# A hybrid decoder step on one core: the sampled tokens' heads in the second token group, earlier fast steps, prefetched head outputs and later pair stores

## The chip, the core and the metric

The kernel runs on one core of a Trainium2 chip. It is one program. Its metric is the device time of one execution in microseconds, as the median of several runs. The core has five engines that run at the same time and wait for each other through semaphores: TensorE (PE in the profile; its weight loads are a row of their own, PEld), VectorE (DVE), ScalarE (ACT), GpSimd (POOL) and SyncE (SP). Each of them works its instructions off in order. SyncE, ScalarE and GpSimd can also issue DMA transfers.

## The reference

One layer of a decoder over 2048 prompt tokens (one sequence) and 8 x 4 sampled tokens with a state of their own, in f32, with a width of 1024:

```python
xn = rms_norm(x, norm_mix_pre)
qk_raw, v_m, o_m, gates, q_a, k_a, v_a = split_projection(xn @ w_in)   # 2312 columns
qk, conv_new = short_conv(qk_raw, conv_buf, conv_w)                    # 4 taps, then silu
# mLSTM heads (4), chunks of 128: matrix memory c, normaliser n, running maximum m
# sliding-window heads (8, in 2 groups of keys), window 128, learned sinks, ALiBi
y_m = mlstm_output(h, o_m, mlstm_norm)
y_a = rms_norm(att, attn_norm)
x = x + rms_norm(concat(y_m, y_a) @ w_out, norm_mix_post)
f = square(relu(rms_norm(x, norm_ffn_pre) @ w_up)) @ w_down            # 4096 wide
x = x + rms_norm(f, norm_ffn_post)
x = x + sigmoid(x @ w_pgate) * (p @ w_pproj)
```

The prompt starts from an empty state. The sampled tokens start from the given state of 8 sequences: c (8 x 4 x 64 x 128), n (8 x 4 x 64), m, the last three rows of the convolution, and caches of 128 keys and values. All outputs and all new states are returned.

## The kernel before

**Numbers.** Each f32 operand of a large matmul is split into a high part and a low part (`split`, `wsplit`: a copy on ScalarE that rounds, then a subtraction on VectorE or GpSimd), and a product is three matmuls, high x high, high x low and low x high (`mm3`). The sampled tokens, 32 rows, have both parts side by side in one operand and need two (`mm2s`).

**Stages.** First the input projection with both kinds of heads, over six chunks of the prompt (`CHUNKS`: four of three blocks of 128 tokens, two of two blocks). The sampled tokens are projected with the last chunk and kept in DRAM (`zsd`). A chunk goes through `gv` (gates, keys and values of the window heads), `qa`, `qk`, `v`, `o`; its mLSTM and window heads run as side work beside the following projections (`mlstm_chunk`, `swa_chunk`) and leave their results in DRAM, `yd`. Then three groups of two chunks each (`GROUPS`) go through output projection (`mix_load`, `mix_mm`, `mix_post`), MLP (`mlp`) and gate (`gate_embed`, `gate_post`, `gate_mm`). The sampled tokens ride along with the last group.

**The MLP.** It has 16 steps of 256 hidden units (`STEPS`). In a plain step `up` takes 96 matmuls for both chunks; in a fast step (`s >= FAST[gi]`, `up_both`) seven products of sums and differences of operand blocks take the place of eight, 84 matmuls. Fast steps need sums of the activations (`sums`, `last_sum`, seven VectorE operations and three splits for each half of the columns), made in step `FAST[gi] - 1`. That step also ends the sampled tokens' heads: `pe.drain(dec)`.

**Weights.** `Ring` hands out weight tiles in the order of one long plan. A tile's f32 data are loaded by SyncE to a raw tile (5 buffers) and split into a pair of high and low part (7 buffers, `PAIRS`). If the plan needs it again, the pair is stored to DRAM by a DMA that GpSimd issues (`keep`), and later loaded back ready-made by SyncE (`get`). In the profile a raw tile is `wr`, a block of `w_up` for the products `wb`, a pair `w`, its copy in DRAM `wk`.

**Order.** TensorE's order is written out: `Flow` keeps a model time of matmuls, and generators (`Side`) emit the next piece of side work when the model time has passed what they yielded; `drain` runs a side to its end. All of TensorE's instructions are held in that order. On the other engines a list scheduler with its own estimates decides the order, so an instruction whose inputs seem ready may be put before earlier ones; `keep_in_program_order` holds one instruction behind the engine's instruction traced before it.

**The sampled tokens' heads.** `decode` is a side of its own: `decode_mlstm`, then `decode_swa`. It is added before the first group's MLP, waits `DECW` = 20 us of model time, and issues its loads from ScalarE (`fetch_small`), one for each of 8 parts of c and 8 of n (L1211, L1212), then bias, queries, keys, values and sinks for the window part (L1259 to L1272). n moves in elements of 4 bytes, in and out (L1254). The two copies of the caches (L1089) are issued by SyncE. The tanh of the output gate is L1226.

**Other places that the change touches.** `fetch` loads and norms the next chunk's tokens (`row_rstd`, L497 to L499; `norm_x`, L584). `weights` in `mlstm_chunk` adds the causal mask to a row that comes back from DRAM (L902, L903). `transpose_x` turns tokens (L149, `ident`), and `split` follows (L227, L228). L1683 adds a `down` product to `f`, L1681 copies the first one, L1647 and L1573 are the sums and the relu of `up`, L1486 and L1488 the evacuation of the output projection, L1392 to L1406 the row norms behind it. `finish` ends in the store L1765.

## Time and profile before

| what | value |
|---|---|
| median of 3 runs | 2689.13 us (2686.86 to 2690.82) |
| the profiled execution | 2687.73 us, its span 2685.6 us |
| mean granted TensorE clock | 0.980 |
| busy: PE, DVE, ACT, POOL | 2546.3, 1473.3, 981.4, 613.3 us |
| moved by DMA | 626.97 MB, mean 233 GB/s |
| input projection with heads | 0 to about 690 us |
| first group: output projection, MLP, gate | from 693, 797 and 1373 us |
| second group: the same | from 1479, 1549 and 2059 us |
| third group: the same | from 2158, 2216 and 2597 us |

All times are us from the start of the span; PE is TensorE's matmuls, an engine's name with q its issuing of DMAs and waits. A row `A <- B: t, n, l` says that A stood t us in total, n times, at the longest l, until B was done. Rows of one line are told apart by tile names: `mo` is the output projection, `up` and `dn` the MLP, `pg` and `pv` the gate, tiles beginning with `dp` and `da` the sampled tokens' heads.

### The profile page before, as it was taken

The page shows a single profiled execution, that of the slowest core. Times are in us where ns is not written, and L with a number is a line of the kernel's source. Part 1 is how long each engine was busy: PE and PEld are TensorE (multiplying, and loading weights), DVE is VectorE, ACT ScalarE, POOL GpSimd, SP SyncE. Part 2 cuts the span into 40 slices and gives each one's busy share as a digit, 9 for nine tenths or more (in the row PEclk, how much of TensorE's full clock was granted, in tenths as well). Part 3 has the DMA queues.
Part 4 walks back from the last instruction along what each step waited for, and adds up shares of the span by engine and source line. Part 5 has one row for each costly group of instructions (what it writes and reads, how often), then busy time and mean ns, then how long its engine had stood idle before and what let it go on. Part 6 is the DMA issues. An engine that isn't in the chain of part 4 may idle for free.

```text
span 2685.6 us, 39181 instructions
## 1 busy us (share of the span) xinstructions
PE 2546.3 (95%) x14282; PEld 2216.1 (83%) x14282; DVE 1473.3 (55%) x3109; ACT 981.4 (37%) x2163; POOL 613.3 (23%) x894
## 2 busy tenths in 40 slices
PE   6899999999878999999989999999999998999997
PEld 6788878887657788888878888899988878999986
DVE  5675756755554486566663474444446345444453
ACT  4555444544433443334452352222223133222241
POOL 5311111112323156566651113000001010000010
PEclk9899999999889999999989999999999999999999
DMA  8756656667977366666589865555556886777786
GB/s 284 275 200 197 208 175 220 210 212 250 287 247 156 133 218 244 235 235 235 227 301 323 322 213 182 187 190 189 188 189 224 293 327 215 255 259 256 258 293 227
DMA packets 225336, 626.97 MB, mean 233 GB/s; under 512 B 35233, under 2 KB 71445, under 8 KB 225128
## 3 DMA queue, kind: packets, MB, share of 16 engines
q1 hardware_dynamic: 173424, 466.78, 52.2%
q0 software_dynamic: 44176, 154.25, 14.8%
q10 hardware_dynamic: 7544, 3.44, 0.6%
q8 instruction: 113, 1.85, 0.3%
q14 instruction: 79, 0.65, 0.1%
HBM read 470.22 MB, written 155.25 MB: 233 GB/s over the span
## 4 chain that ended last, share of the span: by engine, by line
PE 72%; DMA 9%; DVE 8%; issue 4%; POOL 3%; ACT 3%; ACTq 0%; SPq 0%; POOLq 0%; DVEq 0%
PE up L145 19%; PE dn L145 19%; PE pg L145 6%; PE mo L145 4%; PE v L145 3%; PE o L145 2%; PE qk L145 2%; DMA wk<-w 2%; PE gv L145 2%; POOL w L249 2%; PE pv L145 1%; PE aT L149 1%; PE aO L145 1%; DMA w<-wk 1%; PE qa L145 1%
## 5 line engine op out<-in xcount | busy, mean ns | idle before, releaser
L145 PE MATMUL dn<-w,hh 128*128 128x512 f32 x1792 | 567.7, 398 | 14.1 <-DVE f L1683 8.9
L145 PEld LDWEIGHTS dn<-w,hh 128*128 128x128 f32 x1792 | 332.7, 189 | 96.7 <-DVE f L1683 15.4
L1683 DVE TENSOR_TENSOR f<-f,dn 128x512 f32<-128x512 f32 x420 | 285.7, 686 | 218.0 <-PE dn L145 217.7
L145 PE MATMUL dn<-w,hl 128*128 128x512 f32 x896 | 354.3, 395 | 0.1
L1647 DVE TENSOR_TENSOR re<-up,re 128x384 f32<-128x384 f32 (+1 forms) x280 | 144.1, 515 | 297.6 <-PE up L145 297.6
L145 PEld LDWEIGHTS dn<-w,hl 128*128 128x128 f32 x896 | 168.9, 189 | 39.9 <-DVE hl L228 0.6
L268 POOL DMA_DIRECT2D wk<-w x242 | 134.1, 555 | 145.6 <-DVE w L249 109.6
L1648 ACT COPY re<-up 128x384 f32<-128x384 f32 (+1 forms) x40 | 17.9, 448 | 383.1 <-PE up L145 383.1
L228 DVE TENSOR_TENSOR hl<-re,hh 128x384 fp32r<-128x384 f32 (+1 forms) x192 | 117.5, 612 | 65.6 <-ACT hh L227 62.0
L1573 ACT ACTIVATE re<-re 128x384 f32<-128x384 f32 (+1 forms) x160 | 78.8, 493 | 179.3 <-DVE re L1647 177.2
L248 ACT CAST w<-wb 128x512 fp32r<-128x512 f32 x98 | 60.8, 621 | 199.2 <-PE dn L145 124.9
L248 ACT CAST w<-wr 128x512 fp32r<-128x512 f32 (+1 forms) x152 | 93.4, 619 | 104.9 <-issue 30.8
L249 POOL TENSOR_TENSOR w<-wr,w 128x512 fp32r<-128x512 f32 (+1 forms) x76 | 102.0, 1342 | 81.8 <-ACT w L248 62.8
L1394 POOL TENSOR_TENSOR f<-f,gffn 128x512 f32<-128x512 f32 x16 | 21.0, 1319 | 415.4 <-ACT j L1392 415.2
L249 POOL TENSOR_TENSOR w<-wb,w 128x512 fp32r<-128x512 f32 x70 | 89.9, 1295 | 100.8 <-ACT w L248 100.3
L249 DVE TENSOR_TENSOR w<-wr,w 128x512 fp32r<-128x512 f32 (+1 forms) x76 | 80.5, 1061 | 44.4 <-ACT w L248 42.4
L1574 ACT ACTIVATE re<-re 128x384 f32<-128x384 f32 (+1 forms) x192 | 94.8, 494 | 5.9
L1002 DVE CUSTOM_DVE_ANT_0 s<-aS,cst,sink 128x256 f32<-128x256 f32 (+1 forms) x128 | 57.1, 472 | 72.4 <-PE aS L145 72.2
L145 PE MATMUL up<-ut00h,w 128*128 128x384 f32 x320 | 88.6, 348 | 8.4 <-ACT f L1681 5.0
L227 ACT CAST hh<-re 128x384 fp32r<-128x384 f32 (+1 forms) x192 | 92.4, 482 | 6.8
L145 PE MATMUL up<-ut01h,w 128*128 128x384 f32 x320 | 89.8, 343 | 4.8 <-ACT re L1573 4.8
L1008 ACT ACTIVATE s<-s,swt 128x257 f32<-128x257 f32 (+1 forms) x128 | 63.3, 496 | 71.6 <-DVE swt L1005 70.4
(1501 smaller groups left out, 6436.3 us busy)
## 6 DMA issues: line engine op xcount, KB each, us to landing
w<-wk SPq DMA_DIRECT2D x678, 512.0 KB, 4.6
wk<-w POOLq DMA_DIRECT2D x238, 512.0 KB, 5.7
wr<-in_w_down_dram SPq DMA_DIRECT2D x64, 256.0 KB, 5.9
wb<-in_w_up_dram SPq DMA_DIRECT2D x28, 512.0 KB, 3.9
w<-wk SPq DMA_DIRECT2D x20, 528.0 KB, 4.2
x<-in_x_prompt_dram SPq DMA_DIRECT2D x16, 512.0 KB, 4.1
xr<-in_x_prompt_dram SPq DMA_DIRECT2D x16, 512.0 KB, 12.7
y<-yd SPq DMA_DIRECT2D x32, 256.0 KB, 6.2
```

Source lines behind the costliest of these rows:

```text
L145: ins = self.pe.matmul(out, lhsT, rhs, start=start, stop=stop)
L227: act.copy(hi, src)
L228: dve.tensor_tensor(lo, src, hi.bitcast(F32), ALU.subtract)
L248: act.copy(hi, src)
L249: (eng or weng()).tensor_tensor(lo, src, hi.bitcast(F32), ALU.subtract)
L268: put(self.kept[key], t.bitcast(U32))
L1002: dve.tensor_tensor_reduce(s_[:, s, lo : 2 * P], pS[:, s, lo:], bias[:, j, lo:], 1.0 if s == 0 else 0.0625, sink[:, h : h + 1], ALU.add, A ...
L1008: act.activation(e_, e_, AF.Exp, bias=nm[:, s : s + 1], accum_out=sm[:, s : s + 1])
L1573: act.activation(t, src, AF.Relu)
L1574: act.square(t, t)
L1647: add = lambda out, a, b: dve.tensor_tensor(out, a, b, ALU.add)
L1683: dve.tensor_tensor(out(i), out(i), ps[i], ALU.add)
```

## The change

- `FAST` goes from (4, 2, 2) to (2, 2, 2): the first group's MLP takes fast steps from its third step on.
- `decode` is added at the start of the second group's output projection, with `DECW` = 5. Its loads and the cache copies are issued by GpSimd. n is loaded and stored in rows and turned by one transpose each way. The output gate's tanh is held in program order.
- The last chunk's `o` projection loads the head outputs of the first three blocks, transposes and splits them, in place of a `mix_load` that is drained after the projections.
- A pair is stored to DRAM when two more pairs have been taken (`STORE`), in program order on GpSimd.
- The first chunk's further tokens are loaded right behind the first block and normed block by block between the projections; `row_rstd` of token norms and the mask addition are held in program order.
- The query weights of the window heads (`pairs`) come with two transfers, not four, and are split in two halves.
- In the second and third group the second column half of the sums' differences runs on GpSimd.
- `gate_embed` loads all its inputs first and waits 3 us of model time before it turns them.
- The last chunk's outputs are stored by SyncE.
- `LOOK` and `LOOKR`, both 0, are gone.

```diff
-FAST = 4, 2, 2
+FAST = 2, 2, 2
-DECW = 20.0
+DECW = 5.0
-LOOK = 0
-LOOKR = 0
+STORE = 2
+EMBW = 3.0
-    dma, put, fetch_small = nc.sync.dma_start, nc.gpsimd.dma_start, nc.scalar.dma_start
+    dma, put = nc.sync.dma_start, nc.gpsimd.dma_start
+    here = tc.keep_in_program_order
...
         def keep(self, key, t):
             self.kept[key] = dram.tile(list(t.shape), U32, name=f"{self.nm}k{len(self.kept)}")
-            put(self.kept[key], t.bitcast(U32))
+            self.later.append((self.n, key, t))
+
+        def store(self):
+
+            while self.later and self.later[0][0] + STORE <= self.n:
+                _, key, t = self.later.pop(0)
+                here(put(self.kept[key], t.bitcast(U32)))
...
             t = self.tile(n)
+            self.store()
...
                 raw = self.load(512)
-                v = raw.rearrange("p (k j s c) -> p k j s c", k=2, j=2, s=2)
                 for s, src in enumerate(segs):
-                    for k in range(2):
-                        dma(v[:, k, :, s], src[:, k].rearrange("p (j c) -> p j c", j=2))
-                wsplit(h, l, raw)
+                    dma(raw.rearrange("p (k s n) -> p k s n", k=2, s=2)[:, :, s], src)
+                v = raw.rearrange("p (k s j c) -> p k j s c", k=2, s=2, j=2)
+                h, l = (t.rearrange("p (k j s c) -> p k j s c", k=2, j=2, s=2) for t in (h, l))
+                for k in range(2):
+                    wsplit(h[:, k], l[:, k], v[:, k])
...
-        act.activation(junk[:n, :dim], x, AF.Square, accum_out=t[:n, 0:1])
-        dve.tensor_scalar(t[:n, 1:2], t[:n, 0:1], 1.0 / dim, EPS, ALU.mult, ALU.add)
-        pool.tensor_tensor(t[:n, 2:3], t[:n, 1:2], nhalf[:n], ALU.pow)
+        pin(act.activation(junk[:n, :dim], x, AF.Square, accum_out=t[:n, 0:1]))
+        pin(dve.tensor_scalar(t[:n, 1:2], t[:n, 0:1], 1.0 / dim, EPS, ALU.mult, ALU.add))
+        pin(pool.tensor_tensor(t[:n, 2:3], t[:n, 1:2], nhalf[:n], ALU.pow))
...
         if ci == 0:
             norm_x(xq[0], P, "x0")
+            for b in blocks[1:]:
+                xq[b] = load_x(xp[b * P : (b + 1) * P, :], P, f"x{b}")
...
             transpose_x(x, blocks, i, 1, ps_mm)
+            if ci == 0 and i + 1 < nb:
+                norm_x(xq[blocks[i + 1]], P, f"x{blocks[i + 1]}")
...
+            if nm == "o":
+                if last:
+                    ys = [load_y(xpool, "x", b) for b in nxt]
+                else:
+                    fetch(ci + 1)
...
                     if k > 3 and k - 4 < len(nxt):
-                        transpose_x(chunk, nxt, k - 4, 0, ps_m)
+                        if last:
+                            mix_heads(chunk, k - 4, nxt[k - 4], ys[k - 4])
+                        else:
+                            transpose_x(chunk, nxt, k - 4, 0, ps_m)
...
+        if last:
+            for i, t in enumerate(ys):
+                mix_windows(chunk, i, t)
...
-            dve.tensor_tensor(Wt, Wt, bc(mask, 1, MH), ALU.add)
+            here(dve.tensor_tensor(Wt, Wt, bc(mask, 1, MH), ALU.add))
...
-            tc.keep_in_program_order(dma(oc[:, 0 : WIN - DT, :], cc[:, DT:WIN, :]))
+            here(put(oc[:, 0 : WIN - DT, :], cc[:, DT:WIN, :]))
...
             for h in range(MH):
-                fetch_small(cs[er, :, h, 0:128], c_in[e, h])
-                fetch_small(cs[er, :, h, 128], n_in[e, h])
+                put(cs[er, :, h, 0:128], c_in[e, h])
+            for k in range(DB // 2):
+                put(nrow[k * MH : (k + 1) * MH, e], n_in[e, k])
+        yield 1.5
+        pn = psum(ps_s, "dpn")
+        pe.transpose(pn[:, 0:16], nrow.rearrange("p e d -> p (e d)"), ident[:16, :16])
+        dve.tensor_copy(cs[:, :, :, 128], pn[:, 0:16].rearrange("p (k h) -> p k h", k=4))
...
-        act.activation(so, so, AF.Tanh, scale=0.5)
+        here(act.activation(so, so, AF.Tanh, scale=0.5))
...
-    tsp.add(mix_load(0, 0, GROUPS[0][0], False))
-    pe.drain(tsp)
+    yt[0] = chunk
     tsp.add(mix_load(0, 1, GROUPS[0][1], False))
...
     dec = pe.side()
-    dec.add(decode())
...
+                eng = pool if q and gi > 0 else dve
-                dve.tensor_tensor(t1, b12[0], b11[0], ALU.subtract)
+                eng.tensor_tensor(t1, b12[0], b11[0], ALU.subtract)
...
-        put(dst, o[:n])
+        (dma if last else put)(dst, o[:n])
...
-        for i, b in enumerate(c):
-            t = gw.tile([P, PD], F32, tag="p", name=f"p{b}")
+        ts = [gw.tile([P, PD], F32, tag="p", name=f"p{b}", bufs=CMAX + 1) for b in (*c, "s")[: len(c) + sample]]
+        for t, b in zip(ts, c):
             dma(t, pp_in[b * P : (b + 1) * P, :])
+        if sample:
+            dma(ts[-1][:NS], ps_in)
+        yield EMBW
+        for i, (t, b) in enumerate(zip(ts, c)):
             transpose_split(t, ph[:, :, cols(i)], pl[:, :, cols(i)], ps_m, f"pt{b}")
...
             gpost = gain(A["norm_mix_post"], f"gpost{gi}")
+            if gi == 1:
+                dec.add(decode())
             mix_mm(*part[0])
```

More of the change, by code (lines that the diff above doesn't have):

```diff
@@ L1071, in decode_mlstm @@
         cb = sp.tile([P, NCB], F32, name="cb")
[L1072 removed]
+        put(cb, A["const_b"][:, 0:NCB])
         mask_s = cb[:, 0:32]
@@ L1253, in decode_mlstm @@
                 put(c_out[e, h], cs[er, :, h, 0:128])
-                put(n_out[e, h], cs[er, :, h, 128])
+        ncol = sp.tile([P, 16], F32, name="snc")
+        dve.tensor_copy(ncol.rearrange("p (k h) -> p k h", k=4), cs[:, :, :, 128])
+        yield 1.5
+        pn = psum(ps_s, "dpno")
+        pe.transpose(pn[:16, 0:P], ncol, ident)
+        dve.tensor_copy(nrow.rearrange("p e d -> p (e d)"), pn[:16, 0:P])
+        for e in range(2):
+            for k in range(DB // 2):
+                put(n_out[e, k], nrow[k * MH : (k + 1) * MH, e])
     def decode_swa(sp):
@@ L1442, in mix_load @@
             yt["s"] = sp2.tile([P, KT, 2 * NS], F32R, tag="s", name="sy2")
[L1443 removed]
+        todo = [(i, b, load_y(lp, "ld", b)) for i, b in enumerate(c)]
         if sample:
[L1445 to L1448 removed]
+            todo.append((None, "s", load_y(lp, "ld", "s")))
         yield MIXW
[L1450 removed]
+        for i, b, t in todo:
             if i is None:
@@ L1755, in post_ffn, with finish @@
         residual(b, rs, x)
-    def finish(b, half, pg, pv, n, nm):
+    def finish(b, half, pg, pv, n, nm, last):
         hs = slice(half * 512, half * 512 + 512)
```

91 lines of the change are left out of this document (45 added, 46 removed).

## The prediction

> **What bounds the kernel now.** I read the page first, then busy time by stretch, then what TensorE waited for in each stretch, and last the chain of waits where a wait was long.
>
> ```profile
> span 2685.6 us, 39181 instructions
> PE 2546.3 (95%) x14282; PEld 2216.1 (83%) x14282; DVE 1473.3 (55%) x3109; ACT 981.4 (37%) x2163; POOL 613.3 (23%) x894
> ```
>
> TensorE is the bound: 95% busy, no other engine over 55%. So an edit pays in two ways only: fewer matmuls, or less of the 139 us in which TensorE stands. Three stretches show where it stands (columns: stretch, its length, then busy time and instructions of PE, weight loads, DVE, ACT, POOL; granted clock, DMA share, GB/s):
>
> ```profile
> 756.00:790.00 34.00, 13.99 (x52) 10.20 (x51) 10.72 (x39) 9.47 (x20) 6.09 (x6) 0.71 0.61 198
> ...
> 849.00:880.00 31.00, 17.76 (x85) 16.60 (x83) 0.69 (x1) 3.31 (x7) 10.22 (x14) 0.83 0.98 221
> ...
> 1479.00:1549.00 70.00, 70.00 (x323) 57.30 (x322) 32.99 (x60) 24.77 (x52) 12.62 (x15) 1.00 0.88 319
> ```
>
> The first two lie in the first token group, where the sampled tokens' heads run; TensorE idles 20 and 13 us there. The third is the output projection of the second group, where they will run: no idle time, POOL 18% busy, ACT 35%. Now the waits of TensorE by cause (total, times, longest, us), in order of time:
>
> ```profile
> PE x10t L149 <- DVE x L584: 2.6, 1, 2.6
> PE gv L145 <- DVE x0l L228: 1.8, 2, 1.6
> PE aT L149 <- DVE s L1012: 10.7, 1, 10.7
> ...
> PE yt0t L149 <- DMA y<-yd: 2.5, 1, 2.5
> PE mo L145 <- ACT yt00h L235: 1.9, 2, 1.2
> ...
> PE mo L145 <- DMA w<-wk: 13.4, 1, 13.4
> PE mo L145 <- ACT f L1486: 6.6, 1, 6.6
> ...
> PE up L145 <- ACT f L1681: 5.0, 1, 5.0
> PE up L145 <- ACT re L1573: 4.8, 1, 4.8
> PE up L145 <- POOL w L249: 3.4, 1, 3.4
> ...
> PE pt5t L149 <- DMA p<-in_p_prompt_dram: 3.3, 1, 3.3
> PE pt2t L149 <- DMA p<-in_p_prompt_dram: 2.2, 1, 2.2
> ```
>
> These twelve rows are 58.2 us, and the change touches the place of each.
>
> **The sampled heads, part one: what leaves the first group.** Why do matmuls `mo` and `up` wait there?
>
> ```profile
> SPq L274 <- DMA scs<-in_state_mlstm_n_dram: 26.9, 3, 23.3
> ...
> ACT sso L1226 <- DMA w<-wk: 17.0, 1, 17.0
> ...
> L1212 ACTq DMA_DIRECT2D scs<-in_state_mlstm_n_dram x8: 603/627/632, 753.6 to 766.8; - x8
> ...
> ACT re L1573 <- DMA wk<-w: 18.5, 1, 18.5
> ```
>
> The state loads are issued by ScalarE, 0.63 us each; SyncE's weight load stands 23.3 us behind one of them, and ScalarE itself stands 17.0 us in front of a tanh (`sso`) whose input has not landed, so the PSUM copies L1486 queued behind it are late too. The 18.5 us row is the second case: ScalarE sits among the attention cache's loads (L1259 to L1272) while L1573 is due. After the change these loads are issued by POOL, the tanh is pinned behind earlier work, and all of it runs one group later. Removed: 13.4+6.6 = 20.0 us in the projection and 5.0+4.8+3.4 = 13.2 us in the first two MLP steps. The weight making of that stage stays and may leave a little of both: I take **19** (12 to 22) and **12** (6 to 15). The heads' own matmuls move whole, so they add to the second group what they take from the first: 0.
>
> **Part two: what it costs in the second group.** New order on POOL at the seam of the two heads: 8 state stores, 8 normaliser stores, then 9 loads of the attention part, in one queue.
>
> ```profile
> L1254 POOL DMA_DIRECT2D out_dram<-scs x8: 620/620/691, 832.0 to 860.9; - x8
> ...
> DMA to landing us min/median/max: 9.2/12.8/18.1
> ...
> y<-yd SPq DMA_DIRECT2D x32, 256.0 KB, 6.2
> ```
>
> The last number of the lowest row is the time to landing. 25 issues at 0.62 us are 15.5 us, and the loads need up to 6 us more to land; the program allows 15 us of matmuls before the first transpose needs them. 15.5 + 6 - 15 = 6.5 us of waiting. Behind the same issues on POOL queue the row norm's power (L1406) and the gain product (L1394) of the second mix chunk, which the transposes before `up` need; I put 2.5 us, four issues, on that. Together **-9**. Bounds: 0 (all loads float early, POOL is idle there) and -33.2 (every wait of the first group follows). The normaliser's 4-byte stores, which land after 12.8 us, become rows made by two transposes: some tenths of a us on PE, and the DMA share of 0.98 beside only 221 GB/s in 849 to 880 should not come back. Cache copies go from SyncE to POOL, so they no longer stand ahead of weight loads.
>
> A rule of the Trainium skill speaks against this part: DMA: Bandwidth & Descriptors, section SWDGE vs HWDGE vs iDMA, gives plain transfers to the SP and ACT queues and only irregular ones to GpSimd, since its descriptors are written by software. The rows here say otherwise for issue cost: 0.62 us on POOL, 0.63 us on ScalarE. By the rule this part would cost what rival (a) gives it; by the rows, the value taken.
>
> **Two more fast steps.** `FAST` 4 to 2 turns steps 2 and 3 of the first group's MLP from 96 matmuls to 84 for `up`.
>
> ```profile
> 952.65 16.93 PE up L145 x96
> 986.28 12.56 PE up L145 x72
> ...
> 1341.99 14.66 PE up L145 x84
> ...
> 1620.96 14.67 PE up L145 x84
> ...
> 2029.21 14.74 PE up L145 x84
> ```
>
> From the chain of waits: step 3, slow, lasts 986.28-952.65 = 33.6 us; the eleven fast steps from 986.28 to 1341.99 last 32.3 us each, the thirteen of the second group (1620.96 to 2029.21) 31.4. In the first group a fast step still makes and stores its weights, which is the 0.9 us between them. So each converted step saves 1.3 us: **+2.6** (1 to 4.5, the latter if only 16.93-14.67 counted). In the second group these two steps load stored weights instead of making them; they ran without a wait already: 0. The sums' early start (step 1) has the same cover as before.
>
> **First tokens and pinned norms.** The 10.7 us wait of `aT` in the first chunk has this in front of it on DVE:
>
> ```profile
> 68.59 1.28 DVE L584 SCALAR_TENSOR_TENSOR x<-x,x4t,gpre 128x1024 f32<-128x1024 f32 x1
> ...
> 73.14 1.15 DVE L903 TENSOR_TENSOR Wt<-Wt,cst 128x512 f32<-128x512 f32 x1 [1.93 <-DMA Wt<-mbd]
> ```
>
> DVE waited for a mask row (1.93), added it (1.15) and, before, normed next-chunk tokens (1.28 each, three of them) ahead of the softmax's L1012. Pinning takes these off: 1.93+1.15+1.28+1.28 = 5.6, and a third norm some us earlier in part: **+6** (0 to 12). The chain before it on DVE stays. Norming x1 right behind x0's transposes should halve the 2.6+1.8 us: **+2** (-2 to 4). What is late next: norms now come inside the next stage, beside its softmax, in all five later chunks. Transposes come four weight tiles, some 7 us, after the norms' start there, and three norms need 3 x 1.28 us and their chain before them: I take **-2** (-10 to +3). The pair loads' 16 fewer DMA issues and 8 more half-size splits touch no row in which TensorE waits: 0.
>
> **Prefetched head outputs.** From the last `mU` to the first `mo`:
>
> ```profile
> 686.10 1.13 PE L145 MATMUL mU<-vs,kw 128*64 128x130 f32 x8 [0.28 <-DVE num L959]
> 689.75 1.09 PE L149 MATMUL yt0t<-ident,y 128*128 128x128 f32 x4 [2.52 <-DMA y<-yd]
> ...
> 693.19 1.20 PE L145 MATMUL mo<-w,yt00h 128*128 128x512 f32 x2
> ```
>
> That is 6 us from the end of the first row to the start of the last, in which TensorE waits for `yd` and transposes; the two `mo` waits of 1.9 us follow. The three sets of four transposes move into the `o` projection, at 1.09 us a set at most. 6 + 1.9 - 3.3 = **4.6** (2 to 8). The cover is the tail of the window heads; the gain halves still fit there.
>
> **Gates' embeddings and the tail.** Loads put ahead remove most of 3.3+2.2: **+4** (-1 to 6). Last stores:
>
> ```profile
> 2679.60 0.51 POOL L1765 DMA_DIRECT2D out_dram<-ots  x1 [2.13 <-DVE ots L1763]
> ```
>
> 6 us follow this issue to the span's end. No row shows a last store from SyncE; I take a third of the 6 us: **+2** (0 to 4). The stores of the half before now stand on SyncE's queue in front of its last weight loads, which is why the lower end is not above 0.
>
> **Later pair stores.** Each stored pair now waits two tiles longer before its store, and its buffer frees that much later.
>
> ```profile
> POOL wk L268 <- DVE w L249: 109.6, 39, 15.2
> ...
> wk<-w POOLq DMA_DIRECT2D x238, 512.0 KB, 5.7
> ```
>
> POOL no longer stands in front of a store whose split is on DVE (109.6 us, 39 times, mostly idle time that costs nothing), but landing (5.7) starts later. In a fast step 11 tiles pass in 32.3 us, 2.94 each; the ring holds 7, so a buffer has 20.6 us. Two tiles (5.9) and a landing fit unless the matmuls hold it long. In the first output projection a tile is used up by 9 matmuls (1.8 us at the slow step's 33.6/168 = 0.2 each), so 7 tiles give 12.6 us and it is tight: **-2** (-10 to +3).
>
> **Half the sums on POOL.**
>
> ```profile
> 1069.49 1.69 DVE L228 TENSOR_TENSOR hl<-re,hh 128x384 fp32r<-128x384 f32 x1 [0.64 <-ACT hh L227]
> ...
> 1069.45 1.29 POOL L305 TENSOR_TENSOR wb<-wb,wb 128x512 f32<-128x512 f32 x1
> ...
> L1596 DVE TENSOR_TENSOR ts<-ut11h,ut10h x2: 953/954/954, 1565.4 to 1573.7; 128x768 f32<-128x768 f32 x2
> ```
>
> Seven DVE operations of 0.95 us go to POOL, there about 1.94 us each (1.29 for 512 columns, so 768 take half as much again), 13.6 us in all; a DVE split beside POOL took 1.69 us for 384 columns. They depend on the step's inputs alone and end under step 1's own matmuls, 33.6 us by the slow step above; without that cover the fast step behind them would wait: **0** (-4 to +2).
>
> **Sum.** 19+12+2.6+6+2+4.6+4+2 = 52.2; less 9+2+2 = 13; net **39.2**. The profiled execution took 2687.7 us (span 2685.6 and 2.1 around it): 2648.5. It is 1.4 under the median of the runs shown, so the prediction is **2650**. With all best ends it would be some 2606, with all worst 2728.
>
> **Rivals.** (a) The stalls follow the heads: -33.2 in place of -9, so 2674. For it: POOL is in order too, and the heads' matmuls hold TensorE's queue; against: 13 us of POOL work in 70. (b) Nothing comes back: costs of 13 vanish, 2637, and with better ends down to 2612. For it: the second group makes no weights in that stretch. (c) **Slower**: the ring of pairs becomes the bound. Place: the 14 fast steps of the first group. If the whole two tiles, 5.9 us, show in each step, 83 us are lost and the time is 2733; it decides from 39/14 = 2.8 us a step, one tile. Against it: half the tiles of a step are made while `dn` runs, with time to spare. (d) The scheduler orders the loads as before and waits merely change name: 2689.
>
> **Chances.** Forecast 0.55, (a) 0.16, (b) 0.18, (c) 0.08, (d) 0.03. A measurement tells 0.2% (5.4 us) from no change: faster 0.88, same 0.04, slower 0.08. The range leaves out (c) and the far ends: 2612 to 2682.
>
> **What would show it.** In the profile after: no `mo` wait on `w<-wk` over 2 us in the first group and ScalarE free of DMA issues; `up` x84 already at the third step; one or two waits of the heads' transposes (`dpq`, `dph`) beside the second group's `mo` and `up`; `aT`'s wait under 6 us. It is wrong if `dn` or `up` in the first group wait for weights each step (a longer step than 32.3), or if `mo` of the second group stretches by more than the heads' own matmuls and 10 us.

## The result, and the profile after

The changed kernel takes 2675.33 us, median of 5 runs (2669.75 to 2676.5), against 2689.13 for the kernel before on the same chip: a ratio of 0.9943, 95% interval 0.9922 to 0.9963. A second set of runs, shown below, gives 0.9968 (0.9955 to 0.9981). So 9 to 15 us were gained where 39 were forecast. The side was right, the size was not. Single executions of four kernels below, the kernel before among them, took 1.5 to 3.3 times their median; the ratios leave them out, and they move a median by 0.5 us at most.

Page of the changed kernel's profile, first lines:

```profile
span 2674.7 us, 39114 instructions
...
PE 2549.5 (95%) x14260; PEld 2212.9 (83%) x14260; DVE 1481.7 (55%) x3112; ACT 975.9 (36%) x2165; POOL 658.0 (25%) x936
```

TensorE still bounds it. Its idle time fell from 2685.6 - 2546.3 = 139.3 us to 2674.7 - 2549.5 = 125.2 us; POOL has 45 us more work. The same stretches as before (stretch, length, busy time and instructions of PE, weight loads, DVE, ACT, POOL; granted clock, DMA share, GB/s): the first group's output projection, the first 22 us of the second group's, the rest of it, and the first MLP step of the third group:

```profile
701.50:775.50 74.00, 72.85 (x330) 58.63 (x329) 42.09 (x75) 34.67 (x73) 32.66 (x40) 0.98 0.83 299
...
1398.00:1420.00 22.00, 12.97 (x54) 10.07 (x53) 7.63 (x26) 3.00 (x5) 11.12 (x23) 0.71 0.60 187
1420.00:1506.50 86.50, 81.76 (x393) 62.06 (x393) 46.77 (x120) 29.66 (x69) 31.90 (x47) 0.96 0.78 250
2197.60:2246.80 49.20, 34.25 (x193) 30.72 (x192) 32.46 (x50) 19.38 (x43) 16.47 (x15) 0.79 0.54 187
```

The first group's projection has hardly any idle time left, as forecast. The second group's, which ran 70 us without a gap, now has 9 us of idle time in its first 22, at a clock of 0.71, and 5 more after: it lasts 108.6 us for 70.6, and 13.8 of them are idle. That is a sign of being wrong that the prediction named, a stretch by more than the heads' own matmuls and 10 us. The last row is the step into which the third group's sums run; the prediction put their cost at nothing. TensorE's waits by cause (total, times, longest):

```profile
PE aT L149 <- DVE s L1047: 9.5, 9, 2.1
PE dph L149 <- DMA hrow<-in_state_mlstm_conv_dram: 9.0, 1, 9.0
...
PE spv L145 <- DVE qk1se L560: 4.1, 1, 4.1
...
PE dpU L145 <- DVE skm L1275: 2.4, 1, 2.4
...
PE dpX L145 <- issue: 2.3, 1, 2.3
...
PE mo L145 <- DMA w<-wk: 1.4, 2, 0.7
```

The `mo` wait on `w<-wk` is 1.4 us for 13.4, and the waits of `up` on ScalarE and POOL are gone. `aT` waits 9.5 us on this cause in nine small pieces, in place of 12.0 in four, of which one was 10.7. New are `dph` (the heads' first transposes) and `spv` (the sample chunk).

To see where time went, I cut each trace at the start of the first matmul of a stage, read in the timeline. All lengths in us, the changed kernel's from its first profile, the last column that of the last kernel tried; A: start to the first `mo`; B: to the first group's fifth MLP step; C: to the second group's `mo`; D: to its third MLP step; E: to the third group's `mo`; F: to its third MLP step; G: to the end.

| | before | changed | before, no heads | changed, no heads | the same, sums on DVE | heads in first group | ScalarE loads | last version |
|---|---|---|---|---|---|---|---|---|
| A | 693.2 | 701.5 | 692.5 | 693.3 | 695.7 | 698.6 | 698.6 | 690.4 |
| B | 292.9 | 213.6 | 226.0 | 215.2 | 213.5 | 255.0 | 215.0 | 213.4 |
| C | 492.6 | 482.9 | 491.9 | 481.2 | 482.7 | 485.0 | 482.7 | 483.5 |
| D | 142.1 | 201.5 | 142.0 | 155.4 | 142.1 | 156.0 | 213.2 | 183.1 |
| E | 537.4 | 539.3 | 536.9 | 537.7 | 538.1 | 538.5 | 539.3 | 539.4 |
| F | 121.9 | 132.1 | 121.0 | 130.8 | 121.8 | 130.5 | 132.1 | 121.2 |
| G | 405.5 | 403.9 | 403.6 | 404.0 | 403.8 | 403.9 | 403.9 | 404.1 |

B gains 79.3 and C 9.7; D gives back 59.4, F 10.2, A 8.3. The experiments ask what each of these is.

### The profile page after: what moved, and what is told of

It is laid out like the page before. It is cut to its first block, busy times and chain, and to the rows that moved or that the text cites. A ratio compares the mean times of both kernels' runs of the same rounds, so it can differ in the third digit from the quotient of the medians.

```text
span 2674.7 us, 39114 instructions
## 1 busy us (share of the span) xinstructions
PE 2549.5 (95%) x14260; PEld 2212.9 (83%) x14260; DVE 1481.7 (55%) x3112; ACT 975.9 (36%) x2165; POOL 658.0 (25%) x936
## 4 chain that ended last, share of the span: by engine, by line
PE 74%; DVE 10%; DMA 6%; issue 4%; POOL 3%; ACT 2%; SPq 0%; POOLq 0%; DVEq 0%; ACTq 0%
PE dn L145 20%; PE up L145 20%; PE pg L145 5%; PE mo L145 5%; PE v L145 3%; DMA wk<-w 3%; PE qk L145 2%; DVE hl L229 2%; DMA w<-wk 2%; PE o L145 2%; PE gv L145 2%; PE qa L145 1%; PE aT L149 1%; PE aO L145 1%; PE pv L145 1%
## 5 line engine op out<-in xcount | busy, mean ns | idle before, releaser
L1692 DVE TENSOR_TENSOR re<-up,re 128x384 f32<-128x384 f32 (+1 forms) x294 | 152.0, 517 | 326.4 <-PE up L145 326.4
L229 DVE TENSOR_TENSOR hl<-re,hh 128x384 fp32r<-128x384 f32 (+1 forms) x192 | 137.7, 717 | 31.1 <-ACT hh L228 30.4
L250 POOL TENSOR_TENSOR w<-wr,w 128x512 fp32r<-128x512 f32 (+2 forms) x76 | 104.9, 1380 | 87.5 <-ACT w L249 86.6
L249 ACT CAST w<-wr 128x512 fp32r<-128x512 f32 (+2 forms) x152 | 89.3, 598 | 85.6 <-PE up L145 34.3
L1618 ACT ACTIVATE re<-re 128x384 f32<-128x384 f32 (+1 forms) x192 | 95.1, 495 | 5.9
L1037 DVE CUSTOM_DVE_ANT_0 s<-aS,cst,sink 128x256 f32<-128x256 f32 (+1 forms) x128 | 57.0, 473 | 59.4 <-PE aS L145 59.2
L1624 POOL CAST hh<-hh 128x16 fp32r<-128x16 f32 x32 | 8.0, 249 | 319.0 <-ACT hh L228 319.0
L145 PE MATMUL up<-t0h,w 128*128 128x384 f32 (+1 forms) x336 | 85.1, 320 | 0.0
L145 PE MATMUL up<-t1h,w 128*128 128x384 f32 (+1 forms) x336 | 85.1, 320 | 0.0
```

The lines of the kernel that those rows point to most:

```text
L145: ins = self.pe.matmul(out, lhsT, rhs, start=start, stop=stop)
L229: dve.tensor_tensor(lo, src, hi.bitcast(F32), ALU.subtract)
L249: act.copy(hi, src)
L250: (eng or weng()).tensor_tensor(lo, src, hi.bitcast(F32), ALU.subtract)
L1037: dve.tensor_tensor_reduce(s_[:, s, lo : 2 * P], pS[:, s, lo:], bias[:, j, lo:], 1.0 if s == 0 else 0.0625, sink[:, h : h + 1], ALU.add, A ...
L1618: act.square(t, t)
```

## The experiments

Each was timed beside the kernel before, whose median was 2682.4 to 2684.3 in these sets. An interval of a ratio is mostly about ±0.15%, so two kernels under 5 us apart are not told apart. Differences between kernels below are of medians unless the ratio is named.

### Heads or none, sums on POOL or not

Four kernels and the changed one again. Without heads:

```
-    dec.add(decode())                       # in the kernel before
-            if gi == 1:                     # in the changed kernel
-                dec.add(decode())
+    for e in range(2):                      # in both, where the pools of the MLP open
+        put(yds[e], xs[:, e * 512 : e * 512 + 512])
```

Sums on DVE:

```
-                eng = pool if q and gi > 0 else dve
+                eng = dve
```

> The kernel before without the sampled tokens' two heads (left out: their recurrent head, their window head and the outputs these write; the sampled rows that enter the output projection are replaced by a copy of the input, so the rest of the work keeps its size). It measures all that the heads cost in the first group. Theory A (the prediction's terms): 31 to 33 us of stalls and some 28 us of the heads' own matmuls and transposes, so about 60 us less, near 2629. Theory B (the two traces: from the first output projection to the fifth MLP step the changed kernel is 79 us shorter, 3 of it from the two faster steps): about 76 us less, near 2613.

Measured: 2612.08 us, ratio 0.9739 (0.9725 to 0.9754): the heads cost 71.6 us in the first group, nearer Theory B.

> The changed kernel without the sampled tokens' two heads (left out: the same work as in the run above). It measures all that the heads cost in the second group. Theory A (the prediction's terms): 9 us of waits and some 29 us of their own matmuls, 38 us less than the changed kernel, near 2637. Theory B (the two traces: 59 us longer from the second group's projection to the third MLP step, less some us that belong to the sums on POOL): 50 to 59 us less, 2616 to 2625.

Measured: 2619.39, 0.9767 (0.975 to 0.9783): 54 us in the second group, Theory B. So without the heads the changed kernel is *slower* than the one before without them, by 7 us: something else in the change costs.

> The changed kernel with one part undone: both halves of the fast steps' sums on DVE in all groups. Theory A (the prediction: the half on POOL ends under the step's own matmuls): 0, within 5 us of the changed kernel. Theory B (the two traces: the second MLP step of the third group is 9 us longer with the sums on POOL, and in the second group ScalarE waits three times, 2.8 + 3.4 + 3.4 us, for POOL's sums): 9 to 16 us less than the changed kernel, 2659 to 2667.

Measured: 2659.69, 0.9915 (0.9901 to 0.993), Theory B.

> The changed kernel once more, beside the three below on one chip, so that differences of some us can be told. 0.9943 of the kernel before, about 15 us less.

Measured: 2673.63, 0.9968 (0.9955 to 0.9981). So the sums on POOL cost 13.9 us.

> The changed kernel without the sampled heads (left out as in the earlier two runs) and with both halves of the sums on DVE. With the runs made so far it closes a square: heads or none, sums on POOL or not. Theory A (the two costs add up): without heads the sums on POOL cost the 9 to 15 us that they cost with them, so some 12 us less than the changed kernel without heads. Theory B (the trace without heads shows the second group's first MLP step 51.2 us long where the kernel before has 38.0, and the third group's second step 50.1 for 40.2): the sums cost 13 + 10 = 23 us there, hidden in part behind the heads' own stalls when the heads run, so 23 us less than the changed kernel without heads, near 2597.

Measured: 2600.07, 0.9694 (0.967 to 0.9718): 19.3 us less than with POOL's sums, nearer Theory B. With the heads away, D falls from 155.4 to 142.1 and F from 130.8 to 121.8, 22.3 us together. With the heads running D loses less to the sums, 199.4 us in the changed kernel's second profile for 196.4, and F no less, 131.9 for 121.1.

How can work that "ends under the step's own matmuls" cost that? Timeline of the changed kernel's second profile (span 2670.5; start, length, engine, line, then in brackets the wait before), third group, first MLP step (the expectations above call it the second; it is the first, into which the sums run ahead):

```profile
2219.27 0.71 DVE L1645 TENSOR_TENSOR ts<-ts,ts 128x544 f32<-128x544 f32 x1
...
2221.50 1.77 POOL L1643 TENSOR_TENSOR ts<-ut21l,ut20l 128x544 f32<-128x544 f32 x1 [2.37 <-DVE t0l L1659]
...
2222.09 1.77 DVE L1651 TENSOR_TENSOR ts<-ut20h,ts 128x544 f32<-128x544 f32 x1
...
2230.22 0.39 ACT L1617 ACTIVATE re<-up 128x272 f32<-128x272 f32 x1
...
2232.01 1.81 POOL L1653 TENSOR_TENSOR ts<-ut20l,ts 128x544 f32<-128x544 f32 x1
2233.85 0.65 ACT L1658 CAST t2h<-ts 128x544 fp32r<-128x544 f32 x1 [3.24 <-POOL ts L1653]
2234.40 0.43 ACT L1618 ACTIVATE re<-re 128x272 f32<-128x272 f32 x1
...
2235.38 0.58 PE L145 MATMUL dn200t<-hh,w 128*128 128x288 f32 x1 [4.05 <-issue]
```

ScalarE is in order. Its cast `t2h` waits 3.24 us for POOL's last sum; behind the cast stands the square L1618 of the hidden tile, begun at 2230.22 by the relu; behind that the split, and TensorE's `dn` stands 4.05 us. So a sum that is late on POOL delays work that does not need it, because ScalarE has to pass its cast first. This step lasts 49.3 us for 39.8 with the sums on DVE, and 7.9 of the 9.5 are idle time of TensorE. Beside that, a DVE operation of 0.71 us takes 1.77 when a POOL operation is running. The Trainium skill (SBUF — State Buffer, section Who interferes with whom) says that a DVE instruction with two SBUF inputs and a GpSimd instruction that reads SBUF exclude each other, the second waiting for the first. These rows agree: 1.77 against 0.71. How much of the loss is the casts and how much the longer DVE operations was not separated. With the sums on DVE, the casts of this step wait this long, and the operation that took 1.77 is short again (times called, busy us, mean ns):

```profile
ACT t1h L1658 <- DVE ts L1649: 1.4, 1, 1.4
ACT t0h L1658 <- DVE ts L1645: 1.3, 1, 1.3
ACT t2h L1658 <- DVE ts L1653: 1.1, 1, 1.1
...
L1651 DVE TENSOR_TENSOR ts<-ut20h,ts 128x544 f32<-128x544 f32 x2 | 1.4, 719 | 0.0
```

### The heads' place, or the engine of their loads

The heads back in the first group, loads staying on POOL:

```
-FAST = 2, 2, 2
+FAST = 4, 2, 2
-DECW = 5.0
+DECW = 20.0
     dec = pe.side()
+    dec.add(decode())
...
-            if gi == 1:
-                dec.add(decode())
```

> The changed kernel with one part undone: the sampled heads run in the first group again, from the same point and with the same lead as before, and its fast steps begin at the fifth step; their loads stay with POOL. Theory A: the move was worth 20 + 13 - 9 + 3 = 27 us, so this takes 27 us more than the changed kernel, near 2702. Theory B: the first group lost 76 + 3 and the second gained 50 to 59, so 20 to 29 us more, 2695 to 2704, unless the loads' place with POOL alone frees the first group. Theory C (it is ScalarE's loads that cost in the first group, not the place): within 8 us of the changed kernel, 2670 to 2683.

Measured: 2676.93, 0.9975 (0.9963 to 0.9987), 3 us from the changed kernel: Theory C. In the second run the loads go back to ScalarE and the place stays (`put` becomes `nc.scalar.dma_start` for the heads' loads, 32 by the trace; the text below counts 29):

> The changed kernel with the heads' 29 loads issued by ScalarE again, all else as changed (place, tanh pinned, normaliser as rows, cache copies with POOL). Theory A (what cost was the place in the first group; issuing costs the same 0.62 us on either engine): within 5 us of the changed kernel. Theory B (it is ScalarE's loads that cost: the heads cost 71.6 us in the first group with ScalarE's loads, 57.5 with POOL's, and 56 in the second group with POOL's): 10 to 16 us more than the changed kernel, about the time of the kernel before. Theory C (POOL is worse: its loads stand behind the gate stage's stores, 9.0 us of a transpose's wait): 5 to 10 us less.

Measured: 2687.97, 1.0016 (1.0 to 1.0033): 14.3 us more, Theory B. The waits of that kernel in 1396 to 1520:

```profile
ACT f L1532 <- DMA scs<-in_state_mlstm_c_dram: 10.0, 2, 5.5
...
ACT f L1532 <- DMA skc<-in_cache_swa_k_dram: 8.5, 1, 8.5
...
PE mo L145 <- ACT f L1532: 8.3, 2, 5.6
...
ACT f L1532 <- DMA zqk<-zsd: 5.9, 1, 5.9
```

That is the first group's picture of before in the second group: ScalarE stands among its loads, the PSUM copies L1532 come late, and `mo` waits for them. So these stalls follow ScalarE's loads, not the group. With the sums on DVE too the place was tried once more:

> The changed kernel with two parts undone: the heads in the first group (as in the run with the heads in the first group) and both halves of the sums on DVE. Theory A (the place is worth nothing or a little, as 2676.9 against 2673.6 with the sums on POOL says): about the time of the changed kernel with the sums on DVE, 2657 to 2664. Theory B (the second group's place costs some 15 us more than the first's and the run with the heads in the first group did not show it, because there the sums on POOL hit an uncovered step and cost 13 + 10 us and not 14): 12 to 18 us less than that, 2642 to 2648.

Measured: 2656.86, 0.99 (0.9879 to 0.9921), against 2659.69 with the heads in the second group: Theory A. B's arithmetic fell, since A and B of that trace were 4 and 3 us longer than in the other kernel with the heads first.

Next, what the heads still cost in the second group. In the changed kernel POOL issues their loads in order behind the gate stage's output stores:

```profile
1403.39 0.54 POOL L1810 DMA_DIRECT2D out_dram<-ot  x1 [3.77 <-DVE ot L1808]
1403.95 0.55 POOL L1107 DMA_DIRECT2D cb<-in_const_b_dram  x1
...
1405.50 0.52 POOL L1129 DMA_DIRECT2D hrow<-in_state_mlstm_conv_dram  x1
...
1413.38 0.27 PE L149 MATMUL dph<-ident,hrow 24*128 24x24 f32 x1 [9.03 <-DMA hrow<-in_state_mlstm_conv_dram]
```

The store at 1403.39 waits for its data, so the loads start 6 us after the projection's first `mo` (1397.93); `hrow` lands 7.8 us after its issue, and the program puts the transposes right behind the loads. One more yield moves them:

```
+        yield 12.0
         ph = psum(ps_s, "dph")
```

> The changed kernel with 12 us of matmuls put between the heads' first loads and their first transposes (one yield more in the recurrent head; no work added). Theory A (the transposes' 9.0 us wait for their rows is a price of its own, with the lower clock behind it): 9 to 12 us less than the changed kernel, 2661 to 2665. Theory B (the heads' chain is late as a whole and the wait moves to the next step of it): within 3 us of the changed kernel.

Measured: 2670.75, 0.995 (0.9934 to 0.9965): Theory B, 3 us, which is within the noise. The wait did go: D's projection is 96.8 us long, not 106.6. But the second MLP step is 48.4 for 41.2:

```profile
PE dn L145 <- ACT re L1618: 7.3, 1, 7.3
PE dn L145 <- DVE f L1729: 3.1, 1, 3.1
```

> The changed kernel with three edits: sums on DVE, norms pinned in the first chunk alone, 12 us of matmuls ahead of the heads' first transposes; the heads stay in the second group. If the edits add up: 14 + 9 + 10 us less than the changed kernel, near 2641. If the heads' wait only moves: near 2651.

Measured: 2661.49, 0.9913 (0.989 to 0.9936): the edits do not add up. That second step is where the sums begin, and now also where the heads end. So a third edit, besides the yield and the sums on DVE, lets the sums begin one step later (`FAST = 2, 3, 2`):

> The changed kernel with sums on DVE, 12 us of matmuls ahead of the heads' first transposes, and the second group's fast steps from the fourth step on (so that the sums begin one step after the heads have ended). Theory A (the 10 us that the wait's removal won in the projection came back in the second MLP step because the heads' end and the sums share DVE and ScalarE there): that loss goes, 1.3 us are paid for one more slow step, so 6 to 12 us less than the changed kernel with the sums on DVE alone, 2648 to 2654. Theory B (the heads' chain costs the same wherever it ends): 2659 to 2662.

Measured: 2654.14, 0.9883 (0.9866 to 0.9899), the upper end of Theory A. No trace of it is read; the kernels of the last part contain the same edits.

### The projection: pins, and the sample chunk

Norms unpinned in all chunks (`row_rstd(x[:n], n, D, "x", nm)` without `here`):

> The changed kernel with the token norms' three operations no longer pinned to their place in the written order; the order of loading stays. Theory A (the prediction): pins are worth 6 us in the first chunk and cost 2 in the later five, so 4 us more than the changed kernel. Theory B (the two traces: from the end of the first chunk's value projection to the sample chunk the changed kernel gives up 9 us, in waits for the softmax's division on DVE of 6.1, 6 and 2.1 us): 5 to 9 us less, unless the first chunk's 9 us go with them.

Measured: 2674.82, 0.9971 (0.9959 to 0.9983): no difference. The two halves are there but cancel: the first chunk's output-gate projection starts 9.9 us later than with pins (112.6 for 102.7), and the fourth chunk 1.7 us sooner (377.7 for 379.4). Only the first chunk's norms pinned:

> The kernel above, with the token norms pinned in the first chunk alone (the norms of the later chunks' tokens free again). Theory A (pins are worth nothing anywhere, as the run with all of them free says): 0 against the kernel above. Theory B (that run lost 9 us in the first chunk, at 112.6 against 102.7 us when its output projection starts, and won them back by the third): 7 to 11 us less than the kernel above, 2632 to 2641.

Measured: 2656.08, 0.9898 (0.9878 to 0.9917), 0.8 us from the kernel that it was made from. Theory B fell: free norms of the *second* chunk run ahead into the first, whose output-gate projection starts at 110.4 although its own norms are pinned.

A second staging buffer for the sampled rows:

```
-        t = cv_pool.tile([NS, 512], F32, tag="se", name=nm + "se", bufs=1)
+        odd = nm.endswith("1")
+        t = cv_pool.tile([NS, 256 if odd else 512], F32, tag="so" if odd else "se", name=nm + "se", bufs=1)
```

> The changed kernel with a second staging buffer for the sampled rows' query and key halves, so that the copy of one half no longer waits for the store of the other. Theory A (ScalarE's 2.7 us wait for that store is why the value projection of the sample chunk lasts 25.2 us where the kernel before has 19.4): 4 to 6 us less than the changed kernel. Theory B (the stage is bound by the softmax's and the convolution's operations around it, and the wait only shows where it is full): within 2 us of the changed kernel.

Measured: 2666.39, 0.9931 (0.9916 to 0.9946): 7 us less, Theory A and a little more. In the changed kernel's second profile, 599 to 662 us, the first row below is TensorE's longest wait, the second its cause; both are absent with the second buffer, and the value projection is back at 19.4 us.

```profile
PE spv L145 <- DVE qk1se L560: 4.3, 1, 4.3
...
ACT qk1se L559 <- DMA zsd<-qk0se: 3.0, 1, 3.0
```

### Later stores and prefetched head outputs, each undone

`STORE = 0`:

> The changed kernel with the pair stores issued as soon as a pair is made again (no tiles later), still in the written order. Theory A (the prediction): the later stores cost 2 us, so 2 us less than the changed kernel, from 10 less to 3 more. Theory B (without the heads, the changed kernel's first group has an output projection of 74.6 us for 82.0 and fast steps of 32.0 us for 32.5): 7 to 13 us more.

Measured: 2680.57, 0.9989 (0.9977 to 1.0002): 7 us more, 6 by the ratios (0.9989 against 0.9968), the lower end of Theory B. A fast step of the first group lasts 32.4 us for 31.9, and C is 486.2 us long for 481.7 in the changed kernel's second profile. In 915 to 1300 its `dn` waits for DVE's additions:

```profile
PE dn L145 <- DVE f L1728: 8.5, 10, 1.2
```

With later stores this wait is 2.1 us. Why the additions are on time then, I cannot show; DVE's busy time on them is the same, 95.3 and 97.6 us.

Old loading of the head outputs (the loads and transposes of the first token group go back between the last head step and the projection):

> The changed kernel with one part undone: the first token group's head outputs are loaded and transposed between the last stage of the heads and the output projection, as before. Theory A (the prediction): 4.6 us more than the changed kernel, 2 to 8. Theory B (from the start of the sample chunk's output-gate projection to the first matmul of the output projection both profiled kernels take the same, 40.4 and 40.6 us, so the gain went to the heads' last steps, which set that moment): within 2 us of the changed kernel.

Measured: 2684.69, 0.9989 (0.9976 to 1.0002): 11 us more by the medians, 6 by the ratios; its runs scatter from 2675.9 to 2687.6, so the size is not known better than that. Neither theory names the place: the moment of the first `mo` is the same (702.7 and 701.9), but the projection itself is longer. Rows of the projection with the prefetch undone, then of the changed kernel's second profile, columns as above:

```profile
702.70:783.10 80.40, 75.98 (x331) 59.27 (x330) 46.76 (x80) 35.23 (x69) 29.83 (x37) 0.96 0.90 290
```

```profile
701.90:775.00 73.10, 72.03 (x331) 58.57 (x330) 42.30 (x75) 34.81 (x73) 32.64 (x40) 0.99 0.84 306
```

331 matmuls in both, 7.3 us apart: 3.4 us of idle time, and 4 of busy time at a lower clock. TensorE's rows for the first kernel in 650 to 790:

```profile
PE yt0t L149 <- DMA y<-yd: 3.0, 1, 3.0
PE yt4t L149 <- DMA y<-yd: 2.2, 1, 2.2
```

The first wait ends before the projection starts. The second is inside it: the second chunk's transposes (`yt4t`), whose loads SyncE issues from 701.7 us on (from 689.8 with the prefetch), wait too.

### All together

Sums on DVE, the yield, `FAST = 2, 3, 2`, the second staging buffer:

> The changed kernel with four edits: sums on DVE, 12 us of matmuls ahead of the heads' first transposes, the second group's sums one step later, and the second staging buffer. If they add up as measured: 2654 less 7, near 2647; both edits that were measured to cost (the heads' early wait, the sums' meeting with the heads' end) gone, the second MLP step of the second group is below 36 us where the changed kernel has 41.1. If the staging buffer's gain was in a wait that another stage takes up: 2652 to 2656.

Measured: 2642.65, 0.9854 (0.9837 to 0.9871). TensorE has no wait over 2 us left between 1380 and 1600, and D is 182.8:

```profile
1391.10:1573.90 182.80, 176.93 (x899) 140.88 (x898) 103.64 (x233) 75.56 (x163) 49.90 (x79) 0.99 0.64 205
```

With the yield alone the second step was 48.4; here it is 37.7, with one slow step of 33.6 behind it where a fast one took 31.5. In the run of three edits, with the yield and the sums on DVE but not moved, it was 46.1. So it was mainly the meeting of the heads' end with the sums that took the gain back. Then the later norms, one per weight tile:

```
             xq[b] = load_x(xp[b * P : (b + 1) * P, :], P, f"x{b}")
-            norm_x(xq[b], P, f"x{b}")
...
                 if nm == "o":
+                    if not last and 0 < k <= len(nxt):
+                        norm_x(xq[nxt[k - 1]], P, f"x{nxt[k - 1]}")
```

> The kernel above, with the next chunk's token norms pinned one per weight tile of the output-gate projection (at its second to fifth tile) in place of all at its start. Theory A (three norms in one piece hold DVE in front of the softmax's division, which costs 2.8 to 4.2 us in each of the first three chunks): 6 to 11 us less than the kernel above. Theory B (the operations take DVE's time anyway, one after the other): within 2 us of it.

Measured: 2635.21, 0.9823 (0.9807 to 0.9838): 7.4 us less, Theory A. `aT`'s waits in 90 to 500 us, first the kernel above, then this one:

```profile
PE aT L149 <- DVE s L1048: 6.1, 6, 2.1
```

```profile
PE aT L149 <- DVE s L1048: 1.5, 3, 0.5
```

This version beats the kernel before by 47 us and the changed one by 38.

## Why the prediction was wrong

The runs give a path from before to after: take the heads away (2683.7 to 2612.1), make all other edits but POOL's sums (to 2600.1), put the heads into the second group (to 2659.7), put half the sums on POOL (to 2673.6). In gains: 71.6, 12.0, -59.6, -13.9, together 10.1. The prediction's terms along the same path, with the heads' own work cancelling: 22 for the heads (31 - 9) against 12.0 measured, 17.2 for the other edits against 12.0, and 0 for the sums against -13.9. Of the 29 us that are missing, the sums are 14, the heads 10, the rest 5; some 6 of the heads' 10 are lost in the sample chunk, not in the second group (below).

- **Half the sums on POOL: 0 predicted, -14 measured.** This is the step that failed most, and it failed in kind. It priced POOL's operations at 1.94 us for 768 columns; they took 2.1 to 2.5, and 1.5 to 1.8 for the third group's 544. That is not the error that counts. It asked whether the sums would be ready in time. It did not ask what is queued behind those who wait for them: ScalarE's casts, and behind these the hidden tile. The row that would have warned, DVE's split of 1.69 us beside POOL, was quoted and then given no price.
- **The stalls that leave the first group: 31 predicted.** By the pages of before with and without heads, TensorE's idle time falls from 139.3 to 2614.0 - 2506.2 = 107.8, so 31.5 us: right. The rest of the 71.6 is 40.1 us of busy time.

```profile
span 2614.0 us, 38539 instructions
...
PE 2506.2 (96%) x14071; PEld 2191.3 (84%) x14071; DVE 1452.8 (56%) x3008; ACT 962.2 (37%) x2111; POOL 597.8 (23%) x862
```

- **The cost in the second group: 9 predicted.** The same subtraction for the kernels with the sums on DVE gives (2656.6 - 2545.2) - (2597.7 - 2502.3) = 16.0 us of idle time and 42.9 of busy time, so 16 + 2.8 for 9. Not all of that is in the second group: the first and third row below are the sample chunk's value projection and stretch D with the heads, the second and fourth the same without.

```profile
634.60:660.30 25.70, 21.15 (x111) 15.59 (x110) 6.39 (x28) 6.12 (x18) 5.80 (x14) 0.93 0.63 209
...
636.10:655.40 19.30, 19.30 (x110) 14.57 (x109) 6.14 (x28) 6.15 (x18) 1.14 (x6) 1.00 0.72 255
...
1397.10:1593.50 196.40, 180.64 (x898) 144.98 (x897) 110.62 (x245) 76.73 (x163) 47.48 (x77) 0.95 0.61 202
...
1391.90:1534.00 142.10, 141.04 (x686) 120.74 (x685) 84.93 (x141) 58.07 (x111) 15.72 (x21) 1.00 0.69 246
```

  D holds 54.3 of the 58.9 us, 14.7 of them idle time, and the sample chunk 6.4 (other stretches give 1.8 back). The wait foreseen, 6.5 us at the seam of the two heads, is not in the trace; the one that came is at the first transposes, 9.0 us. The step named POOL's queue but read it at one place only, and took the loads' 15 us of lead, which only the window head has, for the whole. The spans of the two kernels:

```profile
span 2656.6 us, 39119 instructions
...
PE 2545.2 (96%) x14260; PEld 2211.5 (83%) x14260; DVE 1473.9 (55%) x3126; ACT 975.1 (37%) x2165; POOL 623.2 (23%) x922
```

```profile
span 2597.7 us, 38429 instructions
...
PE 2502.3 (96%) x14047; PEld 2186.8 (84%) x14047; DVE 1449.3 (56%) x3022; ACT 957.0 (37%) x2113; POOL 591.9 (23%) x856
```

- **Why the heads gained at all.** The mechanism named, ScalarE standing among its own loads, was right; that the gain came from the other group was not. The place is worth 3 us or less either way, the loads' engine 14. The prediction set the Trainium skill's rule (DMA: Bandwidth & Descriptors, section SWDGE vs HWDGE vs iDMA), plain transfers on the SP and ACT queues, against the rows' equal issue cost. The run with ScalarE's loads decides against ScalarE here: 14.3 us more, because the PSUM copies between its loads are on TensorE's path. SyncE, the other queue of the rule, was not tried for these loads.
- **First tokens and pins: 6 + 2 predicted in the first chunk, -2 after.** The first chunk gained 9.5 us (its output-gate projection starts at 103.3 for 112.8); the later chunks gave all of it back: in the first three the output-gate projection lasts 1.2, 2.8 and 4.2 us longer, and the sixth chunk starts at 578.4 for 578.5. The mechanism of the -2 was right, its size was near its lower bound of -10. Spreading the norms returns 7.4.
- **Prefetched head outputs: 4.6 predicted, 6 to 11 measured.** The place was wrong: the term counted the gap ahead of the first `mo`, which came at the same moment, and not the waits of the second chunk's transposes inside the projection, where 7.3 us are. What lies beyond those 7.3 is not explained.
- **Later stores: -2 predicted, +6 to +7 measured.** The sign was wrong. POOL's 109.6 us in front of splits were put down as idle time that costs nothing; whether they were what cost is not shown. Rival (c), the ring of pairs as the bound, is gone with it: fast steps got shorter.
- **Fast steps: 2.6 predicted.** The third and fourth step of the first group, without heads, last 64.0 for 67.2 us: 3.2. Right.
- **Embeddings and tail: 6 predicted.** Not run alone. Without heads and with sums on DVE, the stretches from a group's last step to the next group's projection change by +3.8 and -1.9, and the one to the end by -0.4: about 1.5 in all. The end did come sooner behind the last store, as the step said: 2674.7 - 2671.9 = 2.8 us from its issue to the end, for 6.0.

```profile
2671.90 0.33 SPq L1810 DMA_DIRECT2D out_dram<-ots  x1
```

- **Not in the sum: the sample chunk, -7.** No line of that stage's staging was changed, but its order shifted, so that a copy met a store of its only buffer. Without the heads the same source did not show it, so the path above has it among the heads.

Rival (a), 2674, has the measured time, and a part of its reason (stalls follow the heads: 16 us of idle time, not 33). That is a coincidence of sums: it knew nothing of POOL's sums, the stores or the pins.

The single terms do not close the account. The heads' 12.7 by the spans (71.6 - 58.9) already hold the sample chunk's loss, so that must not be taken off again; 12.7, 3.2, 9.5 - 9.4, 6 to 11, 1.5, 6 to 7 and -14 add up to 15.5 to 21.5, against the 9 to 15 of the two sets of runs. Edits that are undone one at a time need not add up, and on the path all other edits together gave 12.0. What stays open: why the later stores make DVE's additions timely, and why the place of the heads changes A and B by some us.

## What to carry to other kernels

When work is moved to an idle engine, follow its results to the engine that consumes them, and price what stands behind the consumer in its in-order queue: here 14 us were lost with the heads and 19 without, and casts that waited some 3 us each stood in front of the hidden tile. When a wait has two candidate causes (a place and a queue), undo each alone; here the move that looked like the change was worth 3 us or less, and the issuing engine 14. A wait that is removed under a chain with a later meeting point comes back there until that meeting is moved too.

## What the runs showed of the hardware

- A DVE sum of 128x544 took 1.77 us beside a POOL operation, and 0.72 with the sums on DVE.
- Behind its longest wait TensorE was slower for a while. The second group's projection ran at a granted clock of 1.00 without heads, and at 0.71 in its first 22 us with them, where 9 us were idle. Right behind the 9.0 us wait the clock was 0.50 for 6.7 us, and a matmul of `mo` took 0.63 us there for 0.39 ahead of it (changed kernel, groups of matmuls from 1398.0 to 1405.5 and from 1413.3 to 1416.7, with the stretch of the latter):

```profile
L145 PE MATMUL mo<-w,yt10l 128*128 128x512 f32 x9 | 3.5, 394 | 0.0
...
L145 PE MATMUL mo<-w,yt10l 128*128 128x512 f32 x1 | 0.6, 628 | 0.0
...
1413.30:1416.70 3.40, 3.32 (x15) 2.62 (x15) 2.22 (x14) 0.59 (x1) 2.86 (x6) 0.50 0.28 78
```

  So this wait cost more than its own length; how much of the 40 to 43 us of busy time that the heads add is of this kind was not measured.
- The span ended 2.8 us after the issue of its last store from SyncE, and 6.0 us after one from POOL.
